# FoX values and dilated groups 1 and 2 values of h as one 2x2 block product in seven multiplications; dilated group 0 values alone in the first pass

## The chip, the core and the metric

The kernel runs on one core of a Trainium2 chip, with one launch. The time is the device time of that launch in microseconds (us). A core has five engines that work through queues of their own, each in the order in which its instructions were written: TensorE (PE, matrix products, with PEld for the loading of its stationary operand), VectorE (DVE), ScalarE (ACT), GpSimd (POOL) and SyncE (SP, which here only issues DMAs). An instruction waits at the head of its queue until what it needs is there, and everything behind it waits too.

## The reference, cut to what matters

The reference is a decoder layer on x of 1024 tokens by 1024 channels. The change touches only the value columns of its first projection:

```python
h = rms_norm(x, norm_mix_g[layer])
proj = h @ w_in[layer]                      # q, k, v of 3 dilated groups and of FoX, forget logits, gates
dil = proj[..., :o2].reshape(b, s, 3, N_DIL_GROUPS, HEADS_PER_DIL_GROUP, HEAD_DIM)
fox = proj[..., o2:o3].reshape(b, s, 3, N_FOX_HEADS, HEAD_DIM)
f_logit = proj[..., o3:o4].astype(jnp.float32) + b_fgt[layer]
```

The value columns are 512 for FoX (8 heads of 64), 256 for each of the three dilated groups, and beside them 8 columns of forget logits. Two attentions, gates, an output projection and a SwiGLU feed-forward network follow.

## The kernel before

Every float32 operand of a product is split in two parts, hi (a rounding of it, made by ACT) and lo (the rest, made by DVE: line 97 subtracts hi from the source). A product is three matrix products into one PSUM bank: hi by hi, hi by lo, lo by hi (`mm3`, lines 99 to 102). So each operand costs an ACT and a DVE instruction before PE can use all of it.

The work starts with eight token tiles of 128 rows. `norm_transpose` (line 164) squares and sums a tile on ACT (line 168), forms the reciprocal root on ACT and DVE (lines 148 to 161), scales on DVE (line 170), transposes in eight pieces on PE into two PSUM banks (line 175) and splits each bank into `hT_t`, which holds the transposed h, hi and lo. All later products of the first projection read `hT_t`.

The values come in three sets. In the first pass (the pool `foxv`, lines 385 to 447) the 512 FoX columns are computed tile by tile, `values(i)` behind the norm of tile i+1: 8 steps over the channels, three matrix products each, 512 columns wide (for the first two tiles as two halves of 256). The weights `wv` come in four chunks of 128 columns, so that tile 0 can start with the first two. Then, in the pool `dilv` (lines 490 to 510), come group 0 with the forget logits (`w0`, 264 columns) and groups 1 and 2 (`w12`, 512 columns), each for all eight tiles. Every tile's result is copied out of its bank and stored to DRAM (`vf_dram`, `vd_dram`), to be read by the attentions.

The queries and keys that follow (`projections`, line 290) are already products of 2x2 blocks in seven multiplications. They cut h in four blocks, B11 and B21 (tokens 0 to 511, the first and the second half of the channels) and B12 and B22 (tokens 512 to 1023), and need four combinations of them, T1 to T4. `form` (line 461) makes these on DVE: four times hi plus lo (`back`), four additions or subtractions (`vec`) and four splits (`keep`) for one half of a block's channels, twelve DVE and four ACT instructions, each over 128x1024 elements; it is called twice. In the kernel before it runs while PE is busy with the group 0 and the groups 1 and 2 values, which read `hT_t` alone. The left operands, combinations of weights, are made on POOL (`left_side`, lines 275 to 280).

What sets the order: the program is written in the order of the text, and a scheduler at build time deals it out to the engines' queues; `tc.issue_after` keeps an instruction behind a named one. After that each queue is fixed.

## Time and profile before

| what | value |
|---|---|
| median of 3 runs | 1479.5 us (1477.03 to 1481.39) |
| span of the profiled execution | 1476.9 us |
| what lies around the span, from the median | 2.6 us |
| PE busy | 1442.2 us (98%) |
| DVE busy | 956.6 us (65%) |
| ACT busy | 558.0 us (38%) |
| POOL busy | 488.5 us (33%) |
| HBM read and written | 146.32 MB, 66.06 MB |

The profile gives the span of its execution, from the first instruction to the last, and no total of its own; the total is taken as the span and the 2.6 us by which the median lies over it. A row of the timeline gives the start, the busy time, the engine, the line, the operation, the output and the inputs, the shape, the count and, in square brackets, how long the engine had been idle and what ended that. A matrix product's own time (389 ns at 512 columns) overlaps with that of the next one, so that the pace of PE is read from the distance between starts. Times below count from the start of the span.

### The profile page before, as it was taken

How to read it: one execution, taken by the hardware profiler on the slowest of the kernel's cores; microseconds unless marked ns; L12 is line 12 of the kernel's file. 1: busy time of each engine (PE TensorE's matmuls, PEld its weight loads, DVE VectorE, ACT ScalarE, POOL GpSimd, SP SyncE). 2: the span in 40 equal slices, each digit the busy share in tenths (PEclk: the TensorE clock that was granted, in tenths of full speed). 3: DMA queues.
4: the chain of work that ended last, by engine and by line, in shares of the span. 5: the costliest groups of instructions: out<-in, count | busy, mean ns of one | idle time of the engine just before them, and what ended most of it. 6: DMA issues, size and time to landing. Idle time of an engine off the chain costs nothing.

```text
span 1476.9 us, 18419 instructions
## 1 busy us (share of the span) xinstructions
PE 1442.2 (98%) x6876; PEld 1160.9 (79%) x6876; DVE 956.6 (65%) x1344; ACT 558.0 (38%) x832; POOL 488.5 (33%) x438
## 2 busy tenths in 40 slices
PE   8999999999999999999999989999999999999997
PEld 7897888787676676788888778888888887788886
DVE  6482654449889899836627865555566554876556
ACT  5342332236556423354315332232223323533333
POOL 1002434435433221110146146666666665000000
PEclk9999999999999999999999999999999999999999
DMA  8232444474534461275859232232333334976602
GB/s 229 72 107 71 147 160 126 131 214 123 134 108 114 154 209 43 65 240 160 305 199 341 101 86 79 93 106 95 107 107 107 105 104 135 326 250 214 183 31 100
DMA packets 165785, 213.58 MB, mean 145 GB/s; under 512 B 13760, under 2 KB 115136, under 8 KB 165440
## 3 DMA queue, kind: packets, MB, share of 16 engines
q1 hardware_dynamic: 129376, 119.06, 26.4%
q0 software_dynamic: 15200, 55.07, 10.5%
q10 hardware_dynamic: 21120, 38.28, 8.2%
q8 instruction: 54, 0.88, 0.3%
q14 instruction: 35, 0.29, 0.1%
HBM read 146.32 MB, written 66.06 MB: 144 GB/s over the span
## 4 chain that ended last, share of the span: by engine, by line
PE 79%; DVE 12%; issue 3%; ACT 2%; POOL 2%; DMA 1%; SPq 1%; DVEq 0%; POOLq 0%; ACTq 0%
PE pd L287 33%; PE pd L1211 10%; PE pd L100 6%; PE pd L102 6%; PE pd L101 6%; PE pf L102 3%; PE pf L100 3%; PE pf L101 3%; PE pd L197 2%; PE pd L193 2%; PE pd L194 2%; DVE wl L97 2%; PE pd L685 1%; DVE f L1120 1%; ACT wh L96 1%
## 5 line engine op out<-in xcount | busy, mean ns | idle before, releaser
L287 PE MATMUL pd<-hT_t,wh 128*128 128x512 f32 x856 | 264.9, 391 | 2.4 <-ACT cc L313 0.8
L287 PE MATMUL pd<-tT,wh 128*128 128x512 f32 x768 | 236.1, 389 | 4.0 <-ACT wh L96 4.0
L97 DVE TENSOR_TENSOR wl<-wr,wh 128x1024 fp32r<-128x1024 f32 (+2 forms) x110 | 130.7, 1189 | 134.4 <-ACT wh L96 134.2
L96 ACT ACTIVATE wh<-wr 128x1024 fp32r<-128x1024 f32 (+2 forms) x110 | 95.5, 868 | 277.9 <-PE pd L287 163.5
L287 PEld LDWEIGHTS pd<-hT_t,wh 128*128 128x128 f32 x856 | 159.9, 188 | 39.4 <-DVE sg L1011 4.2
L287 PEld LDWEIGHTS pd<-tT,wh 128*128 128x128 f32 x768 | 144.0, 188 | 34.7 <-ACT wh L96 4.9
L287 PE MATMUL pd<-hT_t,wl 128*128 128x512 f32 x428 | 166.6, 389 | 0.0
L287 PE MATMUL pd<-tT,wl 128*128 128x512 f32 x384 | 148.5, 390 | 0.1
L100 PE MATMUL pf<-hT_t,wh 128*128 128x512 f32 x288 | 114.2, 397 | 1.0 <-ACT wh L96 1.0
L102 PE MATMUL pf<-hT_t,wl 128*128 128x512 f32 x288 | 114.2, 397 | 0.0
L101 PE MATMUL pf<-hT_t,wh 128*128 128x512 f32 x288 | 114.1, 396 | 0.0
L96 ACT ACTIVATE wh<-s 128x1024 fp32r<-128x1024 f32 x58 | 61.5, 1060 | 117.5 <-POOL s L276 87.1
L97 DVE TENSOR_TENSOR ol<-raw,oh 128x1024 fp32r<-128x1024 f32 x64 | 77.3, 1224 | 43.7 <-ACT oh L96 40.3
L275 POOL TENSOR_TENSOR s<-wr 128x512 f32<-128x512 f32 x29 | 56.6, 1951 | 142.5 <-PE pd L101 65.0
L96 ACT ACTIVATE oh<-raw 128x1024 fp32r<-128x1024 f32 x64 | 67.2, 1068 | 91.9 <-PE pd L1211 83.5
L287 PEld LDWEIGHTS pd<-hT_t,wl 128*128 128x128 f32 x428 | 80.4, 188 | 16.7
L97 DVE TENSOR_TENSOR wl<-s,wh 128x1024 fp32r<-128x1024 f32 x58 | 75.4, 1299 | 24.1 <-ACT wh L96 24.0
L1211 PE MATMUL pd<-ol,oh 128*128 128x512 f32 x224 | 87.2, 389 | 0.0
L1211 PE MATMUL pd<-oh,ol 128*128 128x512 f32 x224 | 86.2, 389 | 0.0
L1211 PE MATMUL pd<-oh 128*128 128x512 f32 x224 | 85.2, 390 | 0.7 <-DVE acc L1182 0.7
L958 POOL TENSOR_TENSOR r<-r 128x512 f32<-128x512 f32 x32 | 43.1, 1359 | 124.9 <-DMA r<-in_w_ffn_down_dram 123.6
L287 PEld LDWEIGHTS pd<-tT,wl 128*128 128x128 f32 x384 | 72.1, 188 | 15.3 <-DVE wl L97 0.5
(278 smaller groups left out, 3065.0 us busy)
## 6 DMA issues: line engine op xcount, KB each, us to landing
wr<-in_w_in_dram SPq DMA_DIRECT2D x46, 512.0 KB, 4.4
wr<-in_w_ffn_in_dram SPq DMA_DIRECT2D x44, 512.0 KB, 3.9
raw<-left_dram SPq DMA_DIRECT2D x56, 256.0 KB, 3.9
g_dram<-fst ACTq DMA_DIRECT2D x32, 256.0 KB, 2.4
land<-g_dram SPq DMA_DIRECT2D x16, 512.0 KB, 3.5
r<-in_w_ffn_down_dram SPq DMA_DIRECT2D x8, 1024.0 KB, 10.7
right_dram<-r POOLq DMA_DIRECT2D x8, 1024.0 KB, 5.9
left_dram<-f POOLq DMA_DIRECT2D x8, 1024.0 KB, 4.7
```

What stands on the lines that cost most here:

```text
L96: last_hi[0] = nc.scalar.activation(out=hi, in_=src, func=AF.Copy)
L97: return nc.vector.tensor_tensor(out=lo, in0=src, in1=hi.bitcast(F32), op=ALU.subtract)
L100: nc.tensor.matmul(psum, w.hi, m.hi, start=start, stop=False)
L101: nc.tensor.matmul(psum, w.hi, m.lo, start=False, stop=False)
L102: last_mm[0] = nc.tensor.matmul(psum, w.lo, m.hi, start=False, stop=stop)
L193: nc.tensor.matmul(pt[hh][:], w.hi[:, k], m.hi, start=(k == 0), stop=False)
L194: nc.tensor.matmul(pt[hh][:], w.hi[:, k], m.lo, start=False, stop=False)
L197: nc.tensor.matmul(pt[hh][:], w.lo[:, k], m.hi, start=False, stop=(k == kt - 1))
L275: nc.gpsimd.tensor_tensor(out=s12[:, :4], in0=u1, in1=u2, op=ALU.add)
L287: last_mm[0] = nc.tensor.matmul(bank[:], p, q, start=first and k == 0 and n == 0, stop=k == 3 and n == 2, skip_group_check=True)
L958: nc.gpsimd.tensor_tensor(out=out, in0=p, in1=q, op=ALU.subtract)
L1211: nc.tensor.matmul(bank[:], p, q, start=new and n == 0 and i == 0, stop=n == last and i == 2, skip_group_check=True)
```

## The change

The FoX value columns (V0) and those of groups 1 and 2 (V12), 512 each, become the two columns of a 2x2 block matrix: V0 and V12 by the upper and lower half of the channels. With h as the other 2x2 matrix (tokens by channels) the eight block products become seven: B11, B21, T2, T3, T4, T1 and B22 by seven blocks or combinations of weights. `v_product` is one of them: four PSUM banks (four tiles of 128 tokens), four channel steps, three matrix products of 512 columns, 48 in all. h is the stationary side, as before.

The first pass now has group 0 and the forget logits (264 columns) as its `values(i)`, with `w0` loaded at the start. The whole of `w0` is one operand: the forget columns come through a POOL DMA, the 256 value columns through SP as two chunks. The product of B11 follows `values(3)`, that of B21 follows the norms of tiles 4 and 5, and `values(4)` to `values(7)` follow in the text the norms of tiles 6 and 7. The four weight blocks are loaded in the first pass as `quads`, in two halves of 128x4x2x512. POOL makes the four combinations of them in place (`combos`, 8 instructions of 128x1024) and stores them to `sv_dram`; the later products read them back from there on SP (`load_w` through `v_load`), one product reads a raw block again from w_in. `form` makes T2 first. The partial result of B11 is kept in `c1`, and `v2`, `v3` lie where `w0` was. All value stores are issued by ACT, those of FoX were issued by POOL before. The tiles of T3 and T4 lie where `quads` was in the first pass.

```diff
+    s_ctx = pool_of("vsum", 1, side="right")
+    spool = s_ctx.__enter__()
+    sv_dram = dpool.tile([4, KT // 2, P, HALF], F32, name="sv_dram")
+    V0, V12 = FOX0 + 2 * FOX_W, 2 * DIL_W + 256
...
+    def stage():
+        return spool.tile([P, HALF], F32, tag="vst", name=nm("vst"), bufs=2)
...
+    def v_load(rows):
+        return [load_w(rows[k0:k0 + 2].rearrange("k p c -> (k p) c"), 2, HALF) for k0 in (0, 2)]
+
+    def v_product(banks, stat, ws):
+        new = banks is None
+        banks = banks or [pd() for _ in range(NT // 2)]
+        for k0, w in zip((0, 2), ws):
+            for k in range(2):
+                for t, bank in enumerate(banks):
+                    l, r = stat[:, k0 + k, t * P:(t + 1) * P], w[:, k]
+                    for i, (p, q) in enumerate(((l.hi, r.hi), (l.hi, r.lo), (l.lo, r.hi))):
+                        nc.tensor.matmul(bank[:], p, q, start=new and k0 == k == i == 0,
+                                         stop=k0 == 2 and k == 1 and i == 2, skip_group_check=True)
+        return banks
...
+    w0 = Pair(*[w0pool.tile([P, KT, 264], F32R, tag="w0" + n, name=nm("w0"), bufs=1) for n in "hl"])
+    c1 = vsum("c1")
...
-        wv = load_w(w_in[:, FOX0 + 2 * FOX_W:FGT0], KT, FOX_W, tag="wv", bufs=1, pool=vpool,
-                    chunk=P, rpool=vpool, rbufs=3, shared=2 * P, between=first_tokens)
...
+            pv, st = pd(), stage()
+            for k in range(KT):
+                mm3(pv[:, :264], hT[hh][:, k, c:c + P], w0[:, k], k == 0, k == KT - 1)
+            nc.scalar.activation(out=st[:, :256], in_=pv[:, :256], func=AF.Copy)
+            nc.vector.tensor_tensor(out=lf[:, i, :], in0=pv[:, 256:264], in1=bf[:], op=ALU.add)
+            nc.scalar.dma_start(out=vd_dram[0, i], in_=st[:, :256])
...
+        def combos(n):
+            g1, g2, u1, u2 = [quads[n][:, i] for i in range(4)]
+            for to, out, p, q, op in ((3, u2, u1, u2, ALU.add), (2, u1, g1, u1, ALU.subtract),
+                                      (0, g1, u2, g1, ALU.subtract), (1, g2, g2, g1, ALU.subtract)):
+                nc.gpsimd.tensor_tensor(out=out, in0=p, in1=q, op=op)
+                nc.gpsimd.dma_start(out=sv_dram[to, 2 * n:2 * n + 2].rearrange("k p c -> p k c"), in_=out)
...
+        split(w0.hi[:, :, 256:], w0.lo[:, :, 256:], fgt[:])
+        split(w0.hi[:, :, :P], w0.lo[:, :, :P], raws[0][:])
...
+        norm(0)
+        dummies(6)
+        with tc.issue_after(last_hi[0].ins):
+            split(w0.hi[:, :, P:256], w0.lo[:, :, P:256], raws[1][:])
+        norm(1)
+        values(0)
+        norm(2)
+        values(1)
+        norm(3)
...
+            block(0, i)
...
+        values(2)
+        values(3)
+        with tc.issue_after(last_hi[0].ins), tc.issue_after(last_hn[0].ins):
+            ws = block_pair(0)
+        banks = v_product(None, B11, ws)
+        norm(4)
+        norm(5)
+        with tc.issue_after(last_hi[0].ins):
+            for t, bank in enumerate(banks):
+                nc.scalar.activation(out=c1[:, t], in_=bank[:], func=AF.Copy)
+        with tc.issue_after(last_hi[0].ins), tc.issue_after(last_hn[0].ins):
+            ws = block_pair(1)
+        v_product(banks, B21, ws)
+        for n in range(2):
+            combos(n)
+        norm(6)
+        norm(7)
+        with tc.issue_after(last_hi[0].ins):
+            for t, bank in enumerate(banks):
+                st = stage()
+                nc.scalar.activation(out=st[:], in_=bank[:], func=AF.Copy)
+                fox_out(t, st)
+        for i in range(4, NT):
+            values(i)
...
-        back(f2, B12)
+        back(f1, B12)
+        vec(f3, f1, f3)
         back(f4, B22)
-        vec(f1, f2, f3)
-        keep(T1, f1)
-        vec(f2, f4, f2)
-        keep(T3, f2)
+        vec(f2, f4, f3)
+        lo = keep(T2, f2)
+        if then:
+            with tc.issue_after(lo.ins), tc.issue_after(last_hi[0].ins):
+                then()
...
+    form(0, lambda: ws.extend(v_load(sv_dram[0])))
+    form(2)
+    half_t = NT // 2
+    v2, v3 = vsum("w0l"), vsum("w0h")
...
+    banks = v_product(None, T2, ws)
+    for t, bank in enumerate(banks):
+        joined(v2[:, t], bank, c1[:, t])
+    v_product(banks, T3, v_load(sv_dram[2]))
+    for t, bank in enumerate(banks):
+        joined(v3[:, t], bank, c1[:, t])
+    v_product(banks, T4, v_load(v_rows(V12, 1)))
+    for t, bank in enumerate(banks):
+        st = stage()
+        joined(st[:], bank, c1[:, t])
+        dil_out(t, st)
+    banks = v_product(None, T1, v_load(sv_dram[3]))
+    for t, bank in enumerate(banks):
+        st = stage()
+        joined(st[:], bank, v3[:, t])
+        dil_out(half_t + t, st)
+    v_product(banks, B22, v_load(sv_dram[1]))
+    for t, bank in enumerate(banks):
+        st = stage()
+        joined(st[:], bank, v2[:, t])
+        fox_out(half_t + t, st)
```

The names in the rows below: `hn`, `xt` and `pt` are a tile's scaled rows, its input and its transposed bank; `wr` raw weights, `wh`/`wl` their hi and lo; in the changed kernel `w0_1_105`/`w0_2_106` hold hi and lo of the group 0 weights, `wf_7_120` the raw forget columns. `tT` are T1 to T4 (hi and lo each), `f` the scratch tiles of `form`, `lf` the forget logits, `pd` a PSUM bank.

At the start of the program, the ACT queue before, from the square of tile 0 on; `wr_6_137` and `wr_7_141` are the first two chunks of the FoX weights, `wr_18_182` and `wr_28_215` the other two, `pt_16_160` and `pt_17_167` tile 0, `xt_8_143` tile 1:

```order
L168 ACTIVATE hn_9_145,ss_10_146<-xt_1_104 128x1024
L154 ACTIVATE t_12_149<-ss_10_146,epst_88 128x1
L155 ACTIVATE y_11_148<-t_12_149 128x1
L96 ACTIVATE wh_4_135<-wr_6_137 128x8x128
L96 ACTIVATE hT_t_90<-pt_16_160 128x4x128
L96 ACTIVATE hT_t_90<-pt_17_167 128x4x128
L96 ACTIVATE wh_4_135<-wr_7_141 128x8x128
L168 ACTIVATE hn_19_184,ss_20_185<-xt_8_143 128x1024
L96 ACTIVATE wh_4_135<-wr_18_182 128x8x128
L96 ACTIVATE wh_4_135<-wr_28_215 128x8x128
```

and now, with `wr_8_144` and `wr_9_146` the two chunks of group 0, `pt_21_174` and `pt_22_181` tile 0, `xt_10_152` tile 1:

```order
L168 ACTIVATE hn_14_159,ss_15_160<-xt_4_111 128x1024
L154 ACTIVATE t_17_163<-ss_15_160,epst_88 128x1
L155 ACTIVATE y_16_162<-t_17_163 128x1
L96 ACTIVATE w0_1_105<-wr_8_144 128x8x128
L168 ACTIVATE hn_23_196,ss_24_197<-xt_10_152 128x1024
L96 ACTIVATE w0_1_105<-wf_7_120 128x8x8
L96 ACTIVATE hT_t_90<-pt_21_174 128x4x128
L154 ACTIVATE t_26_200<-ss_24_197,epst_88 128x1
L96 ACTIVATE hT_t_90<-pt_22_181 128x4x128
L96 ACTIVATE w0_1_105<-wr_9_146 128x8x128
```

The square of tile 1 stood behind both splits of tile 0 and of the second chunk; now it stands ahead of them.

On PE, around the last token tile (`hn_99_610` before and `hn_102_639` now is tile 7; `wh_4_135` and `wl_5_136` are hi and lo of the FoX weights), the queue before, in which the FoX values of tile 6 stand around the transposes:

```order
L100 MATMUL pd_109_640<-wh_4_135,hT_t_90 128x512
L101 MATMUL pd_109_640<-wl_5_136,hT_t_90 128x512
L175 MATMUL pt_106_625<-ident_82,hn_99_610 128x128 x4
L102 MATMUL pd_109_640<-wh_4_135,hT_t_90 128x512
L100 MATMUL pd_109_640<-wh_4_135,hT_t_90 128x512
L175 MATMUL pt_107_632<-ident_82,hn_99_610 128x128 x4
L101 MATMUL pd_109_640<-wl_5_136,hT_t_90 128x512
```

and now, from the last products of B21 (weights `wh_91_542` and `wl_92_543`):

```order
L403 MATMUL pd_70_427<-wh_91_542,hT_t_90 128x512
L403 MATMUL pd_70_427<-wl_92_543,hT_t_90 128x512
L403 MATMUL pd_70_427<-wh_91_542,hT_t_90 128x512
L175 MATMUL pt_109_654<-ident_82,hn_102_639 128x128 x4
L175 MATMUL pt_110_661<-ident_82,hn_102_639 128x128 x4
L100 MATMUL pd_119_738<-w0_1_105,hT_t_90 128x264
L101 MATMUL pd_119_738<-w0_2_106,hT_t_90 128x264
```

The last tile's transposes stood among the FoX values, ahead of the 384 products of the other two sets; now they stand behind the last product of B21, ahead of the values of tiles 6 and 7 (`pd_119_738`, `pd_121_767`). Behind those comes this, on PE (`pd_147_862` to `pd_150_865` are T2's banks, `tT_125_802` and `tT_126_803` hi and lo of T2, `wh_135_819` and `wl_136_820` its weights):

```order
L101 MATMUL pd_121_767<-w0_2_106,hT_t_90 128x264
L102 MATMUL pd_121_767<-w0_1_105,hT_t_90 128x264
L403 MATMUL pd_147_862<-wh_135_819,tT_125_802 128x512
L403 MATMUL pd_148_863<-wh_135_819,tT_125_802 128x512
L403 MATMUL pd_149_864<-wh_135_819,tT_125_802 128x512
L403 MATMUL pd_147_862<-wl_136_820,tT_125_802 128x512
L403 MATMUL pd_147_862<-wh_135_819,tT_126_803 128x512
L403 MATMUL pd_148_863<-wl_136_820,tT_125_802 128x512
L403 MATMUL pd_148_863<-wh_135_819,tT_126_803 128x512
```

The first three rows of T2 are hi by hi, and everything behind them waits for `wl_136_820` and T2's lo. On DVE, `form` before, among the splits of the groups 1 and 2 weights (`wv`) and the forget logits:

```order
L97 TENSOR_TENSOR wv_123_713<-wr_126_722,wv_122_712 128x8x128
L97 TENSOR_TENSOR wv_123_713<-wr_127_726,wv_122_712 128x8x128
L467 TENSOR_TENSOR f_146_1172<-hT_t_90 128x1024
L467 TENSOR_TENSOR f_145_1171<-hT_t_90 128x1024
L467 TENSOR_TENSOR f_147_1173<-hT_t_90 128x1024
L503 TENSOR_TENSOR lf_96<-pd_131_814,bf_111 128x8
L503 TENSOR_TENSOR lf_96<-pd_132_842,bf_111 128x8
L467 TENSOR_TENSOR f_144_1170<-f_145_1171,f_146_1172 128x1024
L503 TENSOR_TENSOR lf_96<-pd_133_870,bf_111 128x8
L467 TENSOR_TENSOR f_145_1171<-f_147_1173,f_145_1171 128x1024
L467 TENSOR_TENSOR f_146_1172<-hT_t_90 128x1024
L97 TENSOR_TENSOR tT_113_700<-f_144_1170,tT_112_699 128x1024
```

and now, from the last lo half of tile 7 to the lo of T2's first weights:

```order
L97 TENSOR_TENSOR hT_t_90<-pt_110_661,hT_t_90 128x4x128
L550 TENSOR_TENSOR f_131_808<-hT_t_90 128x1024
L550 TENSOR_TENSOR f_134_811<-hT_t_90 128x1024
L550 TENSOR_TENSOR f_133_810<-f_131_808,f_133_810 128x1024
L550 TENSOR_TENSOR f_132_809<-f_134_811,f_133_810 128x1024
L550 TENSOR_TENSOR f_134_811<-f_134_811,f_131_808 128x1024
L97 TENSOR_TENSOR tT_124_801<-f_133_810,tT_123_800 128x1024
L455 TENSOR_TENSOR lf_96<-pd_115_680,bf_118 128x8
L550 TENSOR_TENSOR f_141_840<-hT_t_90 128x1024
L97 TENSOR_TENSOR tT_126_803<-f_132_809,tT_125_802 128x1024
L550 TENSOR_TENSOR f_133_810<-hT_t_90 128x1024
L97 TENSOR_TENSOR wl_136_820<-wr_137_821,wh_135_819 128x1024
```

Ten instructions over 128x1024 now stand between the last half of tile 7 and the end of `wl_136_820`, and the second half of T2's lo (`tT_126_803`, its second row) stands 26 rows behind that half.

129 lines of the change are left out of this document (61 added, 68 removed).

## The prediction

> **What bounds the kernel now.** First the page's busy shares and its chain that ended last: PE works nearly without a break and carries most of the chain, so time goes only where PE has fewer products or waits longer.
>
> ```profile
> PE 1442.2 (98%) x6876; PEld 1160.9 (79%) x6876; DVE 956.6 (65%) x1344; ACT 558.0 (38%) x832; POOL 488.5 (33%) x438
> ...
> PE 79%; DVE 12%; issue 3%; ACT 2%; POOL 2%; DMA 1%; SPq 1%; DVEq 0%; POOLq 0%; ACTq 0%
> ```
>
> Then the busy time by stretches, cut at the stages: up to the first products, the first pass, the group 0, 1 and 2 values, the start of the queries and keys.
>
> ```profile
> core 0: us, PE busy (x) PEld busy (x) DVE busy (x) ACT busy (x) POOL busy (x), PEclk, DMA share, GB/s
> ...
> 13.78:66.80 53.02, 52.67 (x295) 45.73 (x296) 32.61 (x63) 21.61 (x45) 3.99 (x7) 0.97 0.46 142
> 66.80:133.50 66.70, 66.70 (x385) 59.24 (x384) 35.23 (x40) 20.05 (x28) 0.54 (x1) 1.00 0.26 79
> 133.50:150.00 16.50, 14.60 (x62) 11.13 (x61) 11.40 (x14) 7.09 (x12) 11.33 (x10) 1.00 0.34 98
> ```
>
> Between 13.78 and 133.50 us PE idles 0.35 us; in the next 16.5 us it idles 1.9. The changed region ends at 133.5 us, and behind it the program is the same, so the question is when the changed kernel gets there.
>
> The pace of PE, from the first and last of 192 products of 512 columns and of 192 of 264:
>
> ```profile
> 90.01 0.40 PE L100 MATMUL pd<-wv,hT_t 128*128 128x512 f32 x1
> ...
> 133.31 0.39 PE L102 MATMUL pd<-wv,hT_t 128*128 128x512 f32 x1
> ```
>
> ```profile
> 66.80 0.28 PE L100 MATMUL pd<-w,hT_t 128*128 128x264 f32 x1
> ...
> 89.88 0.28 PE L102 MATMUL pd<-w,hT_t 128*128 128x264 f32 x1
> ```
>
> That is 43.30/191 = 0.227 us and 23.08/191 = 0.121 us each.
>
> **The gain.** Before, 2 x 8 tiles x 24 = 384 products of 512 columns (tiles 0 and 1 of FoX in halves); now 7 x 48 = 336. The 192 of group 0 stay. 48 x 0.227 = **10.9 us less**.
>
> **The start.** These rows show ACT and then PE there, before.
>
> ```profile
> 9.07 1.06 ACT L96 ACTIVATE wh<-wr 128x1024 fp32r<-128x1024 f32 x1 [2.63 <-DMA wr<-in_w_in_dram]
> 10.04 1.07 ACT L96 ACTIVATE hT_t<-pt 128x512 fp32r<-128x512 f32 x2
> ...
> 12.35 1.06 ACT L168 ACTIVATE hn<-xt 128x1024 f32<-128x1024 f32 x1 [0.31 <-DMA xt<-in_x_dram]
> 13.32 0.18 ACT L168 ACTIVATION_READ_ACCUMULATOR hn<-xt 128x1 f32 x1
> ```
>
> ```profile
> 12.10 0.39 PE L100 MATMUL pd<-wh,hT_t 128*128 128x256 f32 x1 [1.71 <-ACT wh L96]
> ...
> 13.78 0.39 PE L101 MATMUL pd<-wl,hT_t 128*128 128x256 f32 x1 [1.29 <-DVE v L148]
> ```
>
> The order now puts the square of tile 1 ahead of tile 0's splits, and tile 1 is again the fifth SP load, so ACT waits for it until 12.35. Then follow, by these rows: square and read-out to 13.5, two short instructions of some 0.2 each like the read-out, tile 0's two splits 1.07, second chunk 1.06: hi at 16.0. DVE's 1.2 for lo (its rows stand below) makes 17.2. Before, PE ran from 13.78: **3.4 us more**. If tile 1 came early, the same sum from the first chunk's end at 10.1 gives 15.0, 1.2 more. A second cost is PE's clock:
>
> ```profile
> 15.00:16.00 1.00, 1.00 (x7) 0.52 1.10 381
> 16.00:17.00 1.00, 1.00 (x6) 0.50 1.01 401
> 17.00:18.00 1.00, 1.00 (x7) 0.50 1.10 304
> 18.00:19.00 1.00, 1.00 (x7) 0.78 1.20 323
> ```
>
> After the thin stretch that begins 1.71 us ahead of 12.10 and ends at 13.78, the granted clock was about a half for 3.4 us, which lost 1.7 us of work. Now the gap is twice as long; I take one more such stretch, **1.6 more** (0 to 1.9).
>
> The Trainium skill, TensorE: Matmul & The Clock Gate, Part 1, has the clock halved after one idle window of about 3.4 us, free-running, until one busy window has passed. The 3.4 us of these rows agree; by it this term would be 1.7, and each later gap of that length would cost as much again.
>
> **The end of the first pass.** Here T2 is needed at once. The rows of `form` before, with the last half tile ahead of them:
>
> ```profile
> 57.61 0.69 DVE L97 TENSOR_TENSOR hT_t<-pt,hT_t 128x512 fp32r<-128x512 f32 x1 [0.21 <-ACT hT_t L96]
> ...
> 81.51 3.49 DVE L467 TENSOR_TENSOR f<-hT_t 128x1024 f32<-128x1024 f32 x3
> ...
> 94.42 2.36 DVE L97 TENSOR_TENSOR tT<-f,tT 128x1024 fp32r<-128x1024 f32 x2
> 96.69 2.36 DVE L467 TENSOR_TENSOR f<-hT_t 128x1024 f32<-128x1024 f32 x2
> ...
> 109.49 1.22 DVE L97 TENSOR_TENSOR tT<-f,tT 128x1024 fp32r<-128x1024 f32 x1
> ```
>
> Two such instructions take 96.69 - 94.42 = 2.27, so 1.14 us each; all of `form` lasted from 81.5 to 110.7, the small adds of the forget logits among it:
>
> ```profile
> L503 DVE TENSOR_TENSOR lf<-pd,bf 128x8 f32<-128x8 f32 x8 | 1.0, 160 | 2.9 <-ACT vst L501 2.9
> ```
>
> It cost nothing, because PE had the 66.7 us of the row above that need no T. That cover is gone. I count from E, the end of B21's product. The last tile's eight transposes stand behind it, narrower than 264 columns, about 1.0 at that pace; hi and lo of the second bank, 0.53 and 0.69 and some 0.3 for handovers, end at E+2.5. The values of tiles 6 and 7 take 48 x 0.121 = 5.8, so PE has work until E+6.8, or about E+8 since their banks are first emptied by ACT. DVE then has, by the order, ten instructions over 1024 elements and one small add up to the lo of T2's first weights: E+2.5 + 11.7 = E+14.2. PE does three products and waits for it. The other 21 of T2's first half take 4.8: E+19.0. T2's second half of lo is DVE's 22nd such instruction: 22 x 1.14 + 0.5 = 25.6, so E+28.1. One of the 22 also waits for ACT, whose queue is held by value stores that wait for their two staging buffers; before, such a wait was
>
> ```profile
> 76.51 0.38 ACT L501 ACTIVATE vst<-pd 128x256 f32<-128x256 f32 x1 [3.33 <-DMA vd_dram<-vst]
> ```
>
> 3.33 us once. ACT now waits so for two or three stores here; half of one falls on DVE, 1.7 (0 to 3.7): E+29.8. Sixteen products remain, 3.6: T2 ends at E+33.5. Without waiting it would end at E+1.0+5.8+10.9 = E+17.7. **15.8 more** (14.1 to 17.8). T3, T4, T1 and B22 then run through: DVE needs 4 x 0.69 for their banks (the width and source of a half tile's lo) and 2 x 1.14 for weights, 5.0 in each 10.9.
>
> **What is moved at no cost.** POOL makes eight combinations of 1024 elements; its rows are for 512:
>
> ```profile
> L275 POOL TENSOR_TENSOR s<-wr 128x512 f32<-128x512 f32 x29 | 56.6, 1951 | 142.5 <-PE pd L101 65.0 <-DVE tT L97 36.6 <-DMA wr<-in_w_in_dram 35.0
> ...
> L276 POOL TENSOR_TENSOR s<-s,wr 128x512 f32<-128x512 f32 x29 | 39.4, 1360 | 1.5
> ...
> L959 POOL DMA_DIRECT2D right_dram<-r x8 | 6.3, 793 | 1.5 <-POOL r L958 1.5
> ```
>
> T2's second weights are the sixth: 6 x 2.7 and five issues of 0.8 are 20 us (27 by the slower row). The blocks they need are the last of about 10 MB on SP. At the rates of these rows
>
> ```profile
> 0.00:10.00 10.00, 8.37 (x58) 8.21 (x59) 2.08 (x5) 3.85 (x6) 2.91 (x11) 1.00 0.88 207
> 10.00:20.00 10.00, 7.00 (x43) 6.36 (x42) 7.63 (x14) 7.18 (x14) 0.28 (x1) 0.83 1.11 335
> 20.00:30.00 10.00, 9.65 (x79) 9.13 (x78) 8.44 (x19) 5.12 (x12) 0.74 (x1) 1.00 0.87 259
> ```
>
> 8.0 MB take 30 us, and they are there by about 37. Store and reload cost about 5 us each by these rows:
>
> ```profile
> left_dram<-f POOLq DMA_DIRECT2D x8, 1024.0 KB, 4.7
> ...
> wr<-in_w_in_dram SPq DMA_DIRECT2D x46, 512.0 KB, 4.4
> ```
>
> So the weights are back at 67 (74 by the slower row). E is about 65: 17.2, four times 2.9 for values, 10.9, two times 2.9, 10.9, seven tiles' transposes of 1.0 and 1.6 for the clock make 65. ACT asks for them at about E+10 = 75. They are hidden by 1 to 8 us. On SP all later weight loads stand behind that reload; on ACT and DVE the splits of T3 and T4 wait for the stores, since these tiles lie on `quads`, with value copies and form's second half behind them; the eighth and last store ends at 37 + 8 x 2.7 + 8 x 0.8 + 5 = 70 (80 by the slower row), and T4's split comes at about E+19 = 84. The 9 MB more of DMA lie where the DMA share is 0.26. The forget load moves from SP to POOL, one issue ahead of the identity matrix. FoX's value stores leave POOL for ACT, which is busy 38%.
>
> **Queries and keys.** PE waited there twice:
>
> ```profile
> 137.23 0.73 PE L287 MATMUL pd<-hT_t,wh 128*128 128x512 f32 x2 [0.81 <-ACT cc L313]
> ...
> 141.27 0.96 PE L287 MATMUL pd<-tT,wh 128*128 128x512 f32 x3 [1.02 <-ACT wh L96]
> ```
>
> The second came of POOL, which waited 65.0 us for PE (its row above) for memory that `dilv` held. That ends; but the decay's DVE and ACT steps now come at the same time. **0.5 less** (0 to 1.8).
>
> **Sum.** -10.9 + 3.4 + 1.6 + 15.8 - 0.5 = +9.4. The profiled span of 1476.9 becomes 1486.3, and with the 2.6 by which the median of the runs, 1479.5, lies over it, 1488.9. I take 1489. The ends of the terms give -10.9 + 1.2 + 0 + 14.1 - 1.8 = +2.6, and -10.9 + 3.4 + 1.9 + 17.8 = +12.2.
>
> **Rivals.**
> *PE never waits for T2* (faster). The products take over as soon as the values end: -10.9 + 3.4 + 1.6 - 0.5 = -6.4, 1473. It needs T2's second lo when PE has done 5.4 us of T2, at E+12.2: 22 instructions in 9.7 us, 0.44 each against 1.14. Nothing in the rows is that fast. Chance 0.05.
> *About no change.* The lower ends together, 1482: tile 1 lands early, no half clock, no store wait. Chance 0.11.
> *A second half clock.* Behind a gap later in the program the clock was
>
> ```profile
> 555.00:555.50 0.50, 0.00 (x0) 1.00 0.00 0
> ...
> 557.50:558.00 0.50, 0.50 (x4) 0.76 0.00 0
> ...
> 564.50:565.00 0.50, 0.50 (x3) 0.92 0.00 0
> ```
>
> at a half from 557.7 to 564.5, 3.4 us of work lost. T2's two waits are 5 and about 7 us, so PE may resume at half speed: 1.7 to 3.4 on top, 1491 to 1492.5. Against it: during the first such stretch PE waits anyway. Chance 0.20. By the Trainium skill's rule on the clock gate (TensorE: Matmul & The Clock Gate, Part 1) the halving would come for certain and cost 1.7: 1490.7.
> *The weights come late.* If the blocks land at 45 and POOL runs at its slower row, they are back at 82, 7 us behind the request: 1496. It decides from 8 us of delay on. Chance 0.09.
>
> The forecast keeps 0.55. What a measurement here can tell from no change is about 0.3%, 4.4 us, so faster is under 1475.1 and slower over 1483.9. Faster 0.05 is the first rival, same 0.11 the second, slower the rest, 0.84. The range 1482 to 1495 leaves out the first and the last rival and part of the second.
>
> **What would show it.** The first product of the values near 16 to 17 us instead of 12.1; three products of T2, then a wait for DVE's `wl`; a wait of 6 to 7 us before the second half of T2, with DVE busy without a break; T3 to B22 without waits; the first query product near 143 us. It is wrong if DVE idles while PE waits there, if SP's reloads end the waits, or if PE's idle time behind B21 is under 10 us.

## The result, and the profile after

The changed kernel takes 1496.15 us (median of 4 runs, 1492.92 to 1497.29), the kernel before 1479.12 us on the same chip (1477.03 to 1481.39): a ratio of 1.0112, 95% interval 1.0097 to 1.0128. It is 17.0 us slower, where 9.4 were forecast (1489, range 1482 to 1495). The direction was right, the size was not. The profiled run is the fastest of the four, 1492.92 us with a span of 1491.2, so the trace explains 14.3 us of span. One execution of b22_staging4 below (1792.06 us) and one of b22_st4_start (2905.45 us) were slow ones, and what is said of these two kernels is of the others.

The page's shares are nearly those of before; PE has 96 instructions fewer (48 products, and the 48 more that came of cutting tiles 0 and 1 in halves):

```profile
PE 1441.6 (97%) x6780; PEld 1154.8 (77%) x6780; DVE 982.6 (66%) x1360; ACT 562.0 (38%) x838; POOL 513.2 (34%) x447
```

The busy times by stretches, cut at the first lo product, at the end of B21's product (E), at the end of T2's, at the first query product, and 16.5 us behind that:

```profile
core 0: us, PE busy (x) PEld busy (x) DVE busy (x) ACT busy (x) POOL busy (x), PEclk, DMA share, GB/s
17.53:70.07 52.54, 50.07 (x288) 44.49 (x289) 34.80 (x55) 21.08 (x46) 27.87 (x16) 0.91 0.55 207
70.07:102.22 32.15, 22.34 (x106) 17.87 (x105) 30.78 (x33) 14.60 (x20) 0.00 (x0) 0.84 0.29 99
102.22:147.21 44.99, 43.99 (x194) 35.77 (x192) 21.44 (x28) 9.44 (x9) 2.95 (x4) 1.00 0.45 141
147.21:163.71 16.50, 14.29 (x52) 10.64 (x53) 12.38 (x18) 6.22 (x10) 6.21 (x5) 0.90 0.38 112
```

PE idles 2.5, 9.8, 1.0 and 2.2 us in the four, and the granted clock is 0.91, 0.84, 1.00 and 0.90; before, these were 0.35 us up to 133.5 and 1.9 behind, at 0.97 and then 1.00. So there are two losses: PE waits 13.2 us more (15.5 against 2.3), and half clock takes some 8 us more of its work from 17.53 us on. Less the 10.9 us of products saved, and with the first lo product 3.7 us later, that is about the 14.3 us. The first query product comes 13.7 us later than before (147.21 against 133.53), and what follows it takes 1344.0 us against 1343.4.

PE's waits in these stretches (in brackets: idle before, and what ended it):

```profile
17.53 0.59 PE L101 MATMUL pd<-w,hT_t 128*128 128x264 f32 x1 [0.67 <-DVE v L148]
...
39.66 0.50 PE L403 MATMUL pd<-wl,hT_t 128*128 128x512 f32 x1 [1.78 <-DVE wl L97]
...
72.33 0.39 PE L100 MATMUL pd<-w,hT_t 128*128 128x264 f32 x1 [1.23 <-ACT vst L529]
...
79.65 0.97 PE L403 MATMUL pd<-wh,tT 128*128 128x512 f32 x3 [1.24 <-ACT wh L96]
84.35 0.80 PE L403 MATMUL pd<-wl,tT 128*128 128x512 f32 x1 [3.73 <-DVE wl L97]
...
94.87 0.55 PE L403 MATMUL pd<-wh,tT 128*128 128x512 f32 x1 [3.61 <-ACT tT L96]
95.22 0.63 PE L403 MATMUL pd<-wl,tT 128*128 128x512 f32 x1
...
147.21 0.73 PE L287 MATMUL pd<-hT_t,wh 128*128 128x512 f32 x2 [0.71 <-ACT wh L96]
149.42 0.50 PE L287 MATMUL pd<-hT_t,wl 128*128 128x512 f32 x1 [1.48 <-DVE wl L97]
...
154.30 0.72 PE L287 MATMUL pd<-hT_t,wh 128*128 128x512 f32 x2 [0.74 <-ACT cc L313]
```

The three products of T2, the wait for `wl`, then the wait ahead of its second half are there as foretold. Behind the second wait the products stand about 0.42 us apart, not 0.227: half clock. Two things were not foretold: the wait of 1.78 us ahead of B11's second row of products, and three waits at the queries, where there were two before (0.81 and 1.02 us). The first has its cause in the rows of DVE and POOL at that place:

```profile
34.75 4.85 DVE L97 TENSOR_TENSOR wl<-q,wh 128x1024 fp32r<-128x1024 f32 x1
39.52 1.21 DVE L550 TENSOR_TENSOR f<-hT_t 128x1024 f32<-128x1024 f32 x1
40.66 3.39 DVE L97 TENSOR_TENSOR wl<-q,wh 128x1024 fp32r<-128x1024 f32 x1
```

```profile
33.78 4.73 POOL L476 TENSOR_TENSOR q<-q 128x1024 f32<-128x1024 f32 x2
...
39.69 3.27 POOL L476 TENSOR_TENSOR q<-q 128x1024 f32<-128x1024 f32 x1 [0.49 <-DVE wl L97]
```

A DVE instruction of this size takes 1.21 us between POOL's combinations and 4.85 or 3.39 beside them. POOL's end at 38.51 and 42.96; DVE's end at 39.60 and 44.05, each 1.09 later. So DVE had stood still until POOL was done. The Trainium skill, SBUF — State Buffer, "Who interferes with whom", says that a DVE instruction with two SBUF inputs contends with a GpSimd instruction that reads SBUF, and that this is an exclusive lock; these rows agree.

### The profile page after: what moved, and what is told of

Same layout as the page of the kernel before. It is cut to its first block, busy times and chain, and to the rows that moved or that the text cites. A ratio compares the mean times of both kernels' runs of the same rounds, so it can differ in the third digit from the quotient of the medians.

```text
span 1491.2 us, 18310 instructions
## 1 busy us (share of the span) xinstructions
PE 1441.6 (97%) x6780; PEld 1154.8 (77%) x6780; DVE 982.6 (66%) x1360; ACT 562.0 (38%) x838; POOL 513.2 (34%) x447
## 4 chain that ended last, share of the span: by engine, by line
PE 80%; DVE 12%; issue 2%; ACT 2%; DMA 2%; POOL 1%; SPq 0%; ACTq 0%; DVEq 0%; POOLq 0%
PE pd L287 33%; PE pd L1306 10%; PE pd L403 5%; PE pd L100 4%; PE pd L101 4%; PE pd L102 4%; PE pf L100 3%; PE pf L102 3%; PE pf L101 3%; DVE wl L97 2%; PE pd L780 2%; PE pd L197 2%; PE pd L194 2%; PE pd L193 2%; PE pd L729 1%
## 5 line engine op out<-in xcount | busy, mean ns | idle before, releaser
L97 DVE TENSOR_TENSOR wl<-wr,wh 128x1024 fp32r<-128x1024 f32 (+2 forms) x116 | 140.8, 1215 | 144.0 <-ACT wh L96 142.8
L96 ACT ACTIVATE wh<-wr 128x1024 fp32r<-128x1024 f32 (+2 forms) x116 | 101.9, 879 | 330.2 <-PE pd L287 164.9
```

The source lines that it names most:

```text
L96: last_hi[0] = nc.scalar.activation(out=hi, in_=src, func=AF.Copy)
L97: return nc.vector.tensor_tensor(out=lo, in0=src, in1=hi.bitcast(F32), op=ALU.subtract)
```

## The experiments

In each, the theory is that of the forecast, `form` without cover behind the last tile, with what the trace added: POOL's combinations hold up DVE, half clock follows the waits, and stores on ACT delay the queries. Times are medians; the kernel before had 1477.8 to 1479.3 beside them.

**no_combos: POOL's combinations left out.**

```diff
-                nc.gpsimd.tensor_tensor(out=out, in0=p, in1=q, op=op)
                 nc.gpsimd.dma_start(out=sv_dram[to, 2 * n:2 * n + 2].rearrange("k p c -> p k c"), in_=out)
```

> Leaves out the eight combinations of weights on POOL (the raw blocks are stored in their place, so four of the seven products get wrong weights); all DMAs and every instruction of the other engines stay. In the changed kernel the lo of the B11 product's weights took DVE 4.85 and 3.39 us beside POOL's combinations, against 1.22 elsewhere; PE waited 1.78 us for it and ran at half clock from 40.4 to 43.7 us. Theory collision: DVE is slowed by POOL. Then the two splits take 1.2 us each, PE does not wait ahead of the B11 product, no half clock at 40 us, the B21 product ends near 66.5 instead of 70.1, and the time is about 3.5 us under the changed kernel's 1496: 1492 to 1493. Rival: the splits wait on the arrival or the reading of the weight blocks themselves; then they stay at 3 to 5 us and the time at 1496.

The raw blocks are stored in place of the combinations. 1490.35 us (1487.79 to 1491.56), 5.8 less, where about 3.5 were expected. The same two splits on DVE, in its timeline:

```profile
31.99 1.21 DVE L97 TENSOR_TENSOR wl<-q,wh 128x1024 fp32r<-128x1024 f32 x1
...
34.26 1.22 DVE L97 TENSOR_TENSOR wl<-q,wh 128x1024 fp32r<-128x1024 f32 x1
```

PE does not wait there, and the first query product comes at 142.06 instead of 147.21. Of these 5.15 us 1.4 are there when B11's product starts (31.72 against 33.14): half clock at the start ended at 20.4 us, not 23.5, before the changed kernel's first combination (30.16). The other 3.7 are, to 0.2, the wait (1.78) and the half clock behind it (1.7). The collision is shown; it costs some 3.7 us in these two traces. It can also eat a sooner start: in t_plain and staging4 B11's product began 0.7 to 0.8 us sooner than in the changed kernel, and its lo came at 39.51 and 39.55 us all the same.

**combos_dve: the combinations on DVE.**

```diff
-                nc.gpsimd.tensor_tensor(out=out, in0=p, in1=q, op=op)
+                with tc.issue_after(first_lo[0].ins):     # the last split of B11's weights
+                    nc.vector.tensor_tensor(out=out, in0=p, in1=q, op=op)
```

> The eight combinations of weights are made by DVE instead of POOL, not before DVE has split the B11 product's weights; their stores are issued by POOL as before. Theory collision: the instructions of DVE in 31 to 50 us go back to their own lengths (1.2 us for a split of 128x1024, 1.3 for the scaling), PE does not wait ahead of B11's lo and keeps its clock there; DVE's eight more instructions, 8 x 1.14 = 9.1 us, lie in the 5 and 8.7 us in which it stood idle (47 to 52 and 62 to 71 us in the changed kernel). 1490 to 1492, as without the combinations (1490.4). Rival: they push back the scaling of tiles 4 to 7, PE waits for that, and the time is 1494 to 1500.

1491.82 us (1489.34 to 1495.70), the first query product at 142.32: within 0.3 us of no_combos. DVE's additional 9.1 us lay in its idle time, as expected.

**t7_mid: tile 7's transposes inside B21's product.**

```diff
-        v_product(banks, B21, ws)
+        v_product(banks, B21, ws, (0,))
...
         norm(7)
+        with tc.issue_after(last_tr[0].ins):
+            v_product(banks, B21, ws, (2,))
```

> The transposes of token tile 7 go on PE between the two halves of the B21 product instead of behind it. In the changed kernel DVE and ACT had been done with tile 7's scaling at 63.6 us and then stood idle for 7.7 and 9.5 us until PE came to these transposes at 70.1. Theory uncovered form: DVE's chain from tile 7 to T2's second lo sets when T2 can run, so everything of it starts 5 to 6 us earlier, PE's waits for T2 (9.8 us, and 3.6 us of work lost to half clock) shrink by about that, and the time is 1490 to 1491. Rival: T2 waits for the weights' stores and reloads or for ACT's stores; then the chain starts earlier and PE waits as long as before: 1496.

1493.49 us (1487.27 to 1493.75). The profiled run, one of the long ones, shows what the collision can grow to. DVE, POOL and PE:

```profile
34.46 12.15 DVE L552 TENSOR_TENSOR f<-hT_t 128x1024 f32<-128x1024 f32 x1
46.54 1.21 DVE L97 TENSOR_TENSOR wl<-q,wh 128x1024 fp32r<-128x1024 f32 x1
```

```profile
34.69 4.74 POOL L476 TENSOR_TENSOR q<-q 128x1024 f32<-128x1024 f32 x2
...
40.12 2.39 POOL L476 TENSOR_TENSOR q<-q 128x1024 f32<-128x1024 f32 x1
...
43.17 2.35 POOL L476 TENSOR_TENSOR q<-q 128x1024 f32<-128x1024 f32 x1
```

```profile
47.81 0.80 PE L403 MATMUL pd<-wl,hT_t 128*128 128x512 f32 x1 [6.44 <-DVE v L148]
```

One instruction of 1.2 us took 12.15: it ends at 46.61, again 1.09 us behind the end of POOL's last (45.52), and the split that PE waits for stands behind it. So this run says nothing against the theory; t7_dve repeats it without the collision.

**t2_first: T2 made for both halves ahead of T1, T3 and T4.**

```diff
+        vec(f4, f4, f1)                    # T3's values, kept for later
...
+        def rest():                        # the splits of T3 and T1, and all of T4
...
+    with tc.issue_after(lo.ins), tc.issue_after(last_hi[0].ins):
+        rest0()
+    rest2()
```

> The forming of T1 to T4 is written so that T2 is made for both halves of the channels before anything of T1, T3 and T4 (three more scratch tiles); the instructions are the same. From tile 7's last lo to T2's second lo stand 15 large DVE instructions instead of 22. Theory uncovered form: 7 x 1.14 = 8 us less of DVE work ahead of T2's second half; PE's second wait (3.61 us and its half clock, 1.7) goes and the first stays: 5 to 7 us less, 1489 to 1491. What is put off, T3's second half, must then not be late in its turn: T3 starts about 95 us and DVE has it by 94 us; if it is late, 2 to 3 us come back. Rival: the second wait is ACT's queue, not DVE's: about 1496.

1494.22 us (1491.77 to 1497.27), 147.32 us at the first query product. PE's waits:

```profile
81.05 2.08 PE L403 MATMUL pd<-wh,tT 128*128 128x512 f32 x4 [4.21 <-ACT wh L96]
83.75 0.80 PE L403 MATMUL pd<-wl,tT 128*128 128x512 f32 x1 [0.62 <-DVE wl L97]
99.39 0.77 PE L403 MATMUL pd<-wh,tT 128*128 128x512 f32 x1 [3.62 <-DVE vs L596]
```

The wait ahead of T2's second half went, as expected; the same 3.6 us came back between T2 and T3, because DVE now read T2's banks late (L596 stands behind what had been put off), and the wait ahead of T2's first product grew from 1.24 to 4.21. The expected 5 to 7 us did not come, which fits a total that is bound by how much DVE has to do, not by the order in which it does it.

**t_plain: no product reads T.**

```diff
-    banks = v_product(None, T2, ws)
+    banks = v_product(None, B12, ws)       # B12 also in place of T3, T4 and T1
```

> The four products of T2, T3, T4 and T1 read the block B12 of h in place of T2, T3, T4 and T1 (so their results are other numbers); T1 to T4 are formed as before, for the queries and keys. It prices what waiting for T costs in all. Theory uncovered form: PE's waits for T2's second half and most of the first go, 3.7 + 3.6 us and 3.7 us of half clock; what stays are the waits for the weights behind form's instructions on ACT and DVE, up to 5 us. 6 to 11 us less than the changed kernel's 1496: 1485 to 1490. Rival: the waits are for weights and stores, not for T: 1494 or more.

1493.87 us (1488.38 to 1495.17), the first query product at 143.71. PE's waits:

```profile
82.59 0.80 PE L403 MATMUL pd<-wl,hT_t 128*128 128x512 f32 x1 [3.73 <-DVE wl L97]
97.26 0.77 PE L403 MATMUL pd<-wh,hT_t 128*128 128x512 f32 x1 [2.24 <-DVE vs L582]
```

A miss again by the median, though this profiled run is the fastest: the first wait stays to the hundredth although nothing of T is needed. The wait of 3.61 us ahead of T2's second half is gone, and one of 2.24 stands behind T2 in its place. The first query product comes 3.5 us earlier than in the changed kernel, but 1.75 of that is there behind B21 already (70.58 against 72.33). So PE waits for what stands behind `form` in DVE's queue, the weights' split and then the reading of the banks, more than for T itself. With t2_first this replaces "PE waits for T2" by "PE waits for DVE, which has `form` to do".

**t7_dve: both, tile 7 early and the combinations on DVE.**

> Tile 7's transposes between the halves of B21's product, and the combinations on DVE. Alone, the first gave nothing in its profiled run, because there DVE took 12.15 us for one instruction of form beside POOL's combinations (34.5 to 46.6 us) and PE waited 6.44 us for the split behind it. With that gone, theory uncovered form has DVE come to form's first instruction 5 to 6 us ahead of combos_dve and T2's waits shorter by as much: 1484 to 1487. Rival: the time is that of combos_dve, since DVE, now with eight more instructions, comes to form no earlier.

1488.89 us (1487.41 to 1493.23) against combos_dve's 1491.82, above the expected 1484 to 1487. PE's waits for T2, in combos_dve and then here:

```profile
80.07 0.79 PE L403 MATMUL pd<-wl,tT 128*128 128x512 f32 x1 [3.70 <-DVE wl L97]
90.58 0.57 PE L403 MATMUL pd<-wh,tT 128*128 128x512 f32 x1 [3.63 <-ACT tT L96]
```

```profile
74.67 0.51 PE L403 MATMUL pd<-wl,tT 128*128 128x512 f32 x1 [0.32 <-DVE wl L97]
...
88.42 0.80 PE L403 MATMUL pd<-wh,tT 128*128 128x512 f32 x1 [4.63 <-ACT tT L96]
```

T2 begins 5.4 us earlier, its second half only 2.2, and the first query product (141.91) 0.4. The gain of 2.9 by the medians is within the spread of the runs; it is not shown to be more than that.

**b22_first and b22_once: B22's product ahead of T2's, in banks of its own.**

```diff
+    own = v_product([pd(), pd(), bank_f(), bank_f()], B22, ws1, new=True)
     banks = v_product(None, T2, ws)
     for t, bank in enumerate(banks):
         joined(v2[:, t], bank, c1[:, t])
+        joined(v2[:, t], own[t], v2[:, t])
...
-    v_product(banks, B22, v_load(sv_dram[1]))
```

> On top of t7_dve, the product of B22, which needs no T, goes ahead of T2's into four banks of its own, and is added to v2 when T2's banks are read (four DVE additions of 128x512 more). Theory uncovered form: PE now has 10.9 us more of work that needs no T between the end of B21 and T2, more than T2's waits were (9.8 us); no wait of over 1 us is left ahead of T2, T3, T4 and T1, the half clock there goes too: 1477 to 1481, about the time of the kernel before, or under it. Rival: the weights of B22 are the last that are stored and read back, so PE and, behind their splits, form wait for them, and part of the wait only moves: 1482 to 1487.

As it was built, b22_first also ran B21's 48 products a second time, each time starting the banks anew, so that B11's share was lost; that is 10.9 us that the expectation did not have: 1490.73 us (1490.28 to 1492.62). T2 waited 0.52 us in it. b22_once is without that.

> As b22_first was meant: the product of B21 runs once (there it ran twice, 48 products or 10.9 us more), tile 7's transposes stand between its halves, the combinations are on DVE, and B22's product goes ahead of T2's. Theory cover: form and the splits keep DVE busy for some 35 us behind tile 7; PE has 5.8 + 10.9 us without T, and T2 itself, against them. In b22_first, with 10.9 us more, T2 waited 0.52 us in all; without them it waits 0 to 6 us. The time is that of b22_first less 10.9, plus 0 to 6 and plus the half clock of one wait: 1480 to 1487. Rival: the wait that comes back eats it all, 1489 or more, as t7_dve.

1484.18 us (1481.43 to 1487.37). Its stretches up to T2's wait, up to the first query product, and behind it; then PE's waits:

```profile
67.00:97.20 30.20, 28.93 (x150) 24.55 (x150) 29.24 (x31) 15.40 (x20) 0.00 (x0) 1.00 0.42 139
97.20:129.94 32.74, 32.73 (x144) 27.13 (x145) 19.12 (x24) 6.13 (x6) 3.46 (x4) 1.00 0.37 115
129.94:146.44 16.50, 7.25 (x24) 5.58 (x23) 8.17 (x17) 2.76 (x6) 2.56 (x3) 0.69 0.55 177
```

```profile
97.21 0.47 PE L403 MATMUL pd<-wh,tT 128*128 128x512 f32 x1 [1.28 <-ACT wh L96]
...
142.07 1.22 PE L287 MATMUL pd<-hT_t,wh 128*128 128x512 f32 x2 [9.25 <-ACT cc L313]
```

With 10.9 us more of PE work beside DVE's, one wait of 1.28 us is left between B21's product and the queries, no half clock, and the first query product comes at 129.94, 3.6 us ahead of the kernel before. That shows the cover to be the cause. DVE is as busy as ever (29.24 of 30.20 us), but nobody waits for it. Then 9.25 us are lost in one wait for ACT's copy of the first bank.

**staging4, b22_staging4: four staging buffers for the stores.**

```diff
+    def stage():
+        return xpool.tile([P, HALF], F32, tag="vs4", name=nm("vst"), bufs=4)
```

> The staging buffers of the stores behind the last token tile are four instead of two, and the scheduler then puts the first split of the query weights on ACT ahead of the last four value stores. In the changed kernel ACT stood idle for 9.94 us ahead of that split (146.10 us), behind store issues that waited for DVE's last additions; PE waited 0.71, 1.48 and 0.74 us at the first query products and lost 1.7 us to half clock. Theory stores: the split comes near 142 us, right behind the first half of B22's products, the waits of 0.71 and 1.48 and the half clock go, and the first query product starts at the same place: 3 to 4 us less, 1492 to 1493. Rival: the wait is for POOL's combinations of the query weights or for the raw loads on SP; then the waits stay within 0.5 us and the time at 1496.

On the changed kernel alone: 1488.88 us (1485.42 to 1490.97), 7.3 less, more than expected. In its trace the waits of 0.71 and 1.48 us are gone and 0.85 us is left, without half clock at the queries. The span is 4.4 us shorter, but 1.7 of that is not the stores' doing: it is there behind B21 already (70.66 us against 72.33), because no half clock followed the wait of 1.77 us at B11 in this run. Some 2.7 are left for the stores; the rest of the 7.3 is open.

> b22_once with four staging buffers. In b22_first PE waited 9.24 us at the first query products (149.7 us), because ACT's copy of the first bank stood behind eight value stores that waited for DVE and for two staging buffers. Theory stores: with four buffers the stores are issued earlier and this wait shrinks to some 2 to 5 us: 4 to 7 us under b22_once, 1475 to 1481. Rival: DVE's eight additions for the last two sets of tiles are what ACT waits for, and the buffers change under 2 us.

1478.39 us (1474.32 to 1483.46), ratio to the kernel before 0.9996 (0.998 to 1.0012): level with it. ACT at the queries:

```profile
132.07 2.66 ACTq L408 DMA_DIRECT2D vf_dram<-vst  x4
...
136.93 0.60 ACT L313 ACTIVATE cc<-pd 128x512 f32<-128x512 f32 x1 [1.53 <-DMA vf_dram<-vst]
```

The copy `cc` still stands behind the store issues, and then waits for a store to land, presumably since its tile lies where the staging buffers were. PE waits 4.49 us.

**start_order, b22_st4_start, x1_early: the start.** The first two put tile 1's square back behind tile 0's splits; the third loads tile 1 one place earlier on SP.

```diff
-        norm(1)
+        with tc.issue_after(last_hi[0].ins):
+            norm(1)
```

> The square of token tile 1 is put back behind tile 0's two splits and the second weight chunk on ACT, as in the kernel before; nothing else moves in the first pass. Theory start: ACT no longer waits 3.14 us for the DMA of tile 1 at 9.7 us, the first product starts at 12 to 13 us instead of 16.3, and the half clock after it is shorter by one stretch: 3.5 to 5 us less, 1491 to 1493. Rival: the weight blocks' DMAs, which land at 29 us, set when the B11 product can start, so that what is won at the start is lost ahead of that product: 1495 to 1496.

1495.52 us (1489.99 to 1497.06): the rival's time, though not shown to be for the rival's reason. PE:

```profile
13.91 0.59 PE L101 MATMUL pd<-w,hT_t 128*128 128x264 f32 x1 [0.87 <-DVE w L97]
23.12 0.39 PE L100 MATMUL pd<-w,hT_t 128*128 128x264 f32 x1 [3.81 <-ACT hT_t L96]
...
33.41 1.20 PE L403 MATMUL pd<-wh,hT_t 128*128 128x512 f32 x4 [0.23 <-ACT wh L96]
```

PE starts 3.6 us earlier, then waits 3.81 us for tile 1 with half clock behind it, and B11's product starts at 33.41, against 33.14 in the changed kernel.

> b22_staging4 with the old order at the start (the square of tile 1 behind tile 0's splits). In the changed kernel the order gave nothing behind tile 1, since the B11 product's weights came at 39.7 us in both. With the combinations off POOL those weights come at 36 us or sooner, so now the start should show: 1 to 3 us under b22_staging4, 1473 to 1479. Rival: tile 1's scaling, which comes later by as much, eats it again: the same time as b22_staging4.

1479.48 us (1477.04 to 1484.28), 1.1 over b22_staging4, with a like wait (2.87 us) for tile 1: no gain either.

**in_place_sp: b22_once with the last additions in place, their stores on SP.**

```diff
-        st = stage()
-        joined(st[:], bank, v2[:, t])
-        fox_out(half_t + t, st)
+        joined(v2[:, t], bank, v2[:, t])
+        nc.sync.dma_start(out=vf_dram[half_t + t], in_=v2[:, t])       # likewise for v3 and vd_dram
```

> b22_once, with the last eight additions made in place in v2 and v3 (no staging buffers) and their eight stores issued by SP, ahead of its next weight loads, instead of ACT. In b22_staging4 PE waited 4.49 us for ACT's copy of the first query bank, which came at 136.9 us, behind eight store issues and behind memory that the staging buffers had held. Theory stores: the copy comes within 1.5 us of the bank's last product (133 us), PE waits 0 to 2 us instead of 4.5 and loses no half clock there (2.8): 4 to 7 us under b22_staging4's 1478.4, 1471 to 1475, faster than the kernel before. Rival: DVE's eight additions, 5.8 us in a row behind the last product, are what the first bank's copy or POOL's combinations wait for, by the memory that they share; then the wait stays at 3 us or more and the time at 1477 to 1479.

1474.90 us (1472.57 to 1480.21), ratio to the kernel before 0.9972 (0.9957 to 0.9986): faster than the changed kernel, and than the kernel before by 0.3%. PE:

```profile
128.97 0.62 PE L287 MATMUL pd<-hT_t,wh 128*128 128x512 f32 x2
132.54 0.73 PE L287 MATMUL pd<-hT_t,wh 128*128 128x512 f32 x2 [0.69 <-ACT cc L313]
139.07 0.73 PE L287 MATMUL pd<-hT_t,wh 128*128 128x512 f32 x2 [2.44 <-ACT wh L96]
```

The wait for `cc` fell from 4.49 to 0.69 us, as the theory said; a new one of 2.44 comes of weight loads that now stand behind the stores on SP.

> in_place_sp with tile 1's input loaded ahead of the second chunk of the group 0 weights. The order of ACT alone (start_order, b22_st4_start) had brought the first product from 16.2 to 13 us, and PE then waited 2.9 to 3.8 us for tile 1 at 23 us. Theory tile 1: what sets the second tile's values is tile 1's arrival and norm, since group 0's 24 products of one tile (2.9 us, 5.8 at half clock) are over before; with tile 1 landing some 1.5 us earlier the values of tile 1 start at 21 to 22.5 us instead of 23 to 24.4, and B11's product and all behind it 1 to 2 us earlier: 1 to 2 us under in_place_sp. Rival: the DMAs behind are bound by bandwidth up to 30 us, so the second chunk comes later by as much, or B11's weights set the pace: no difference.

1475.62 us (1473.50 to 1477.56): no difference. ACT waits 1.52 us for tile 1 ahead of tile 0's splits instead of 3.05, and PE's first product comes 1.3 us earlier (14.90 us), but in both kernels half clock lasts to about 21 us; the first query product comes 0.4 us earlier (128.54). Tile 1's arrival does hold up the first product, and it costs next to nothing.

## Why the prediction missed, step by step

*48 products fewer, 10.9 less:* right. The pace is unchanged: 43.99 us of PE work for the 192 products from T3 to B22 is 0.229 each.

*The start, 3.4 more:* the first lo product came at 17.53, forecast 17.2. The reason was half right. ACT's order does delay the first product, but undoing it gains nothing: with 2.9 us of products for one tile PE then waits for the next.

*Half clock at the start, 1.6 more:* it took 3.3 us of PE's work (half clock from 13.26 to 23.50 us) against 1.7 before, so the size was right. That is partly luck: with the same start it took 1.8 us in no_combos and 3.4 in b22_staging4.

*The end of the first pass, E about 65:* 70.07. That E counts one stretch of half clock where the sum has two, the one of before and one more; with both it is 66.7. The other 3.4 us are where the forecast failed. Under "what is moved at no cost" POOL's eight combinations were priced by one thing, whether the weights come back in time. They did. What they do to DVE meanwhile was put at nothing. It cost the wait of 1.78 us and 1.7 us of work at half clock behind it; no_combos agrees, with 3.7 us less from B11's product on. In t7_mid the wait grew to 6.44 us. The trace of before shows the same thing in small, where it cost the first pass nothing: behind the first queries a DVE instruction of 1.2 us took 2.00 beside POOL, and ended at 152.71, 1.09 us behind POOL's 151.62:

```profile
150.71 2.00 DVE L97 TENSOR_TENSOR wl<-s,wh 128x1024 fp32r<-128x1024 f32 x1 [2.27 <-ACT wh L96]
```

```profile
150.31 1.31 POOL L280 TENSOR_TENSOR s<-wr,s 128x512 f32<-128x512 f32 x1
```

*T2, 15.8 more:* from E to T2's end 32.15 us, forecast 33.5; less the 17.7 without waits 14.4, within its bounds (14.1 to 17.8). The first `wl` came at E+14.3, forecast E+14.2. The second half came 5 us sooner than forecast (94.87 us): PE went on when ACT had made its hi, without waiting for its lo, and DVE, without a break from 71.33 us on, was never held up by ACT's stores. Then 24 products remained, not sixteen (1.8 us), and half clock took 1.7. That these errors nearly cancel is luck. b22_once shows the cause, missing cover; t_plain and t2_first correct its wording: not T2 is late, but DVE has more to do than PE has products, and every order of it makes something late.

*A second half clock (rival, 0.20):* it did come, behind both of T2's waits and also behind the waits at B11 and at the queries. At T2 only the second stretch lengthened anything, by 1.7; during the first PE would have waited anyway, as the prediction argued. By the rule of the Trainium skill (TensorE: Matmul & The Clock Gate, Part 1) one more stretch at T2 gave 1490.7, which stopped short because the other waits were not foreseen; and here less than a whole idle window was enough (last section).

*Queries and keys, 0.5 less:* the wait for POOL's memory went, but 0.71 + 1.48 + 0.74 us of waits and a stretch of half clock (0.90 over 16.5 us is 1.7) against 1.83 before make 2.8 more. Of that 0.7 lies ahead of the first query product; from it to the end the trace takes 0.6 us more, so some 1.5 were made up further on, where is not shown. The forecast looked at POOL and the decay, and not at the value stores, which now stood on ACT just ahead of the query weights. staging4 and in_place_sp show it.

*The upper end, 12.2 more:* it was the sum of the known terms' bounds, and had none for what two engines share: POOL's long two-input instructions beside DVE's, which the trace of before shows only behind the changed region. The rival of late weights did not come true. In the traces the 9.4 are short by 4.9 us: 3.4 at B11, 0.3 at the start, 1.4 from T3 to B22 (44.99 us for 4 x 10.9, with waits of 0.28 and 0.71) and 1.1 at the queries, less 1.4 at T2. What remains open is the 2.7 us by which the medians differ more than these two runs do, since one run of each kernel has a trace.

## What to carry to other kernels

A reordering that saves PE work has to be costed on the engine that prepares its operands: count what that engine must do between two points and what PE has to do beside it, because moving work within its queue only moves the wait. Work put on POOL "because it is idle" is to be laid against DVE's rows at the same time, instruction by instruction. And the last step of a stage, its stores on a queue and its staging memory, is ahead of the first step of the next stage: look what stands behind it. And two single traces of this program can differ by 1.7 us for the place of a wait alone (last section), so a saving of that size is not read from them.

## What the runs showed of the hardware

DVE beside POOL: an instruction over 128x1024 with both inputs in SBUF took 1.21 us alone, 3.39 and 4.85 beside POOL's, and 12.15 across four of POOL's instructions in a row; in all three slow cases it ended 1.09 us after one of them. In the last it got no turn in the gaps of 0.7 us between POOL's instructions. In the changed kernel the splits of PSUM banks in that time kept their length:

```profile
33.55 1.28 DVE L97 TENSOR_TENSOR hT_t<-pt,hT_t 128x512 fp32r<-128x512 f32 x2
```

Half clock: in the changed kernel a wait of 1.78 us brought 3.4 us of it, while no_combos kept the full clock through 3.9 us of idle PE in ten, and t_plain through the same wait of 1.77 us. The length of a wait alone does not tell. In the first 166 us of all sixteen traces every stretch of half clock lasts 3.41 us, or twice or three times that, and those of one trace lie on one grid of 3.41 us, placed differently in each run. Cut at its grid, no piece at full clock in which PE idled up to 1.69 us was followed by half clock, and each with 1.95 us or more was; of the six between, three were. Here are pieces of the changed kernel, in which the wait lies in one, and of t_plain, where it is cut in two (us, PE busy, granted clock, DMA share, GB/s):

```profile
37.16:40.57 3.41, 1.63 (x11) 1.00 0.37 136
40.57:43.98 3.41, 3.41 (x10) 0.50 0.16 61
```

```profile
35.55:38.96 3.41, 2.19 (x19) 1.00 0.16 55
38.96:42.37 3.41, 2.86 (x13) 1.00 0.48 181
```

And the ten of no_combos:

```profile
85.50:95.50 10.00, 6.08 (x26) 4.37 (x25) 9.97 (x10) 4.01 (x4) 0.00 (x0) 1.00 0.18 52
```
